# The low parts of split weights, and the one-hot products of the expert selection, on VectorE in place of GpSimd

## The chip, the cores and the metric

The kernel runs on one core of one Trainium2 chip. The metric is the device time of one execution in microseconds; the time before is the median of three runs. The profile shows one execution, with TensorE as PE (its weight loads as PEld), VectorE as DVE, ScalarE as ACT, GpSimd as POOL and the load queue of SyncE as SP.

## What is computed

One layer of a step for 1024 prompt tokens and 8 samples of 8 tokens, in float32. The mixer splits `xn @ w_in` into a differential attention and a gated recurrence; cross attention over 256 memory tokens follows; then every token picks experts:

```
s = einsum('thcd,hckd->thck', q, sub_keys)
s1, i1 = top_k(s[:, :, 0], 16);  s2, i2 = top_k(s[:, :, 1], 16)
cand_s = s1[..., :, None] + s2[..., None, :]
cand_i = i1[..., :, None] * 128 + i2[..., None, :]
top_s, j = top_k(cand_s, 16)
e = take_along_axis(cand_i, j);  g = softmax(top_s)
act = gelu(einsum('ted,td->te', u[e], x))
out = einsum('te,ted->td', g * act, v[e])
```

There are 8 heads with 16 experts each for a token, out of 16384 experts with one row of 1024 numbers in `u` and one in `v`. The samples also attend to 8192 cached tokens, read by pages.

## The kernel before

The 1024 prompt tokens are eight tiles of 128 (0 to 7), the 64 sample tokens are tile S. Matrix products keep float32 precision by splitting both operands into a high and a low part, and adding three products (high x high, high x low, low x high; L290 to L292). For weights this is done on the fly: `raw` [128, 512] is loaded (L284), ScalarE rounds it to the high part (L276) and GpSimd subtracts the high part from `raw` to make the low part (L277, in `split_w`; L306 for a small block; L1326 for the rows of `v`). `raw` has 3 buffers, `ws` (both parts) has 4.

By the profile's clock the program has three stretches, called **stage 1 to 3** here.

- Stage 1, to about 1590 us: projections and mixing of the first groups of tiles, what follows the mixing for tiles 0 and 1, and beside it the samples' attention over the cache (L755 to L798).
- Stage 2, to about 3393 us: what follows the mixing for tiles 2 to 7 and S (`post_pass`), with the mixing of the last groups beside it, and at its end `gates` (L1246 on), which lays out the gates of tiles 2 to 5 for all experts. In `post_pass` each block of queries ends in `peer_select` (L1006): VectorE finds the best 16 of 50 candidates, compares places with `io50` (L1038, `eq`), GpSimd multiplies this one-hot tile with the candidates' expert numbers (L1041, `oh`), VectorE sums (L1043). That is 8 such products for each tile, 72 in all.
- Stage 3, to the end: `dense` (L1279 on). For tiles 2 to 5 all experts are computed, in 16 groups of 8 blocks of 128 experts. For each block `u` is loaded and transposed on TensorE; ScalarE takes the high part (L249), VectorE the low one (L250); 24 products make the scores `S` (L1302); ScalarE applies gelu (L1306), VectorE multiplies by the gates (L1311), ScalarE and VectorE split the result `H` (L1312, L1313). Then two halves of 512 columns: each loads and splits eight `raw` blocks of `v` (L1325, L1326), TensorE multiplies (L1330), and VectorE adds the four banks to `accd` (L1334).

**The gathers.** For tiles 0, 1, S, 6 and 7 the experts' rows are fetched one slot at a time: GpSimd issues an indirect DMA of 128 rows (L1218, 1152 of them), VectorE multiplies a row of `u` with the token and sums it (L1224), or adds a weighted row of `v` to `acc` (L1231). A gathered tile `g` has 3 buffers before stage 3, and 3 + 2 in it. So the next gather waits until VectorE has finished with an earlier one. They run beside the other work in stages 2 and 3.

**The order.** The program is written as streams that are paced against each other by costs in numbers, and a scheduler turns this into one fixed order of instructions for each engine; every engine works its own order from front to back. Gathers are put behind what GpSimd has been given last:

```
with tc.issue_after(gmark[0]):
    return all(next(gstream, False) for _ in range(n))
```

`gmark[0]` is set to the newest instruction at several places, L277 and L1041 among them; the others are L231, L660 and L1271.

Of the kernel before, what the change touches and what calls it, by code (L numbers as in the profile page):

```python
# [7 lines left out]
F32 = mybir.dt.float32  # L8
# [5 lines left out]
OP = mybir.AluOpType  # L14
AX = mybir.AxisListType

P = 128
# [4 lines left out]
S = 8                                   # index of the sample tile (64 tokens)  # L22
# [3 lines left out]
PSLOT = {S: "s", 0: 0, 1: 1, 2: 2, 3: 3, 4: 0, 5: 1, 6: 2, 7: 3}       # slot of a tile's transposed operands  # L26
GORDER = [0, 1, S, 6, 7]                # experts' rows gathered for these tiles
DENSE = [2, 3, 4, 5]                    # all experts' products for these
RATIO = 1.2                             # the sample's attention per unit of other work
LEAD = 100.0                            # work of group 2 before the sample's attention is done  # L30
GRATE = 0.85                            # gathers per unit of other work,
GSLOW = 0.3                             # while experts are chosen
PCOST, MCOST, GCOST, SCOST = 124.0, 160.0, 160.0, 240.0     # work after the mixing, of mixing, of gates, after it with the sample
# [4 lines left out]
def host_consts():  # L38
# [4 lines left out]
    le = (i[:, None] <= i[None, :]).astype(float)          # [j, i] = j <= i  # L43

    def cum(idx):                                          # columns: sum of j <= idx
        return (i[:, None] <= np.asarray(idx)[None, :]).astype(float)
# [23 lines left out]
    c["caus"] = np.where(i[None, :] > i[:, None], NEG, 0.0)    # [q, k]  # L70
# [35 lines left out]
CSEG = [(0, 16), (1, 8), (2, 5), (3, 4), (4, 3)]          # first rank, how many second ranks  # L106
# [3 lines left out]
def step_kernel(ctx: ExitStack, tc: tile.TileContext, consts, a, outs):  # L110
# [25 lines left out]
    stream = [""]                       # whose PSUM banks are handed out  # L136
# [44 lines left out]
    def bcast(src, n):                  # a DRAM vector on every partition  # L181
        return bass.AP(tensor=src.tensor, offset=src.offset, ap=[[0, P], [1, n]])

    # gains of the q/k norms
# [7 lines left out]
    # gains of normed rows, by feature [partition, block]  # L192
# [11 lines left out]
    # lambda  # L204
# [20 lines left out]
    # ---------------------------------------------------------------- helpers  # L225
    def rstd(pool, ss, n, w, k, tag="rs", bufs=4):
        """(ss / k + eps) ** -0.5 for [n, w]."""
        ms = pool.tile([P, 16], F32, tag="ms", name="ms", bufs=3)
        nc.vector.tensor_scalar(ms[:n, :w], ss, 1.0 / k, EPS, op0=OP.mult, op1=OP.add)  # L229
        r = pool.tile([P, 16], F32, tag=tag, name=tag, bufs=bufs)  # L230
        gmark[0] = nc.gpsimd.tensor_tensor(r[:n, :w], ms[:n, :w], nhalf[:n, :w], op=OP.pow).ins  # L231
        return r

    def row_norm(pool, src, n, out, g=None):
        """out = rmsnorm(src) (* g), rows of 1024."""
# [9 lines left out]
    def split_T(dst, blk, ps, n, w, g=None):  # L245
        """PSUM [128, w blocks, n], times the features' gains, into the parts of a transposed operand."""
# [15 lines left out]
    def make_T(t, src, n, g0=0, ng=2, gn=None):  # L262
        """[n, 512 ng] -> parts [128, 2, 8, n] with features on partitions, from block 4 g0."""
# [8 lines left out]
    def split_w(ws, raw, w, g=None):  # L272
        """Parts of weights [128, w], times their rows' gains."""
# [3 lines left out]
        gmark[0] = nc.gpsimd.tensor_tensor(ws[:, 1, :w], raw, ws[:, 0, :w].bitcast(F32), op=OP.subtract).ins  # L277

    def proj(tiles, T, wsrc, c0, w, consume, gn=None):
        """consume(t, ps) for each tile's [n, w] block of columns from c0."""  # L280
# [18 lines left out]
    def proj_ga(tiles, T, wsrc, c0, consume):  # L299
        """consume(t, ps) with ps [16, n]: the gates' low-rank input with features on partitions."""  # L300
# [5 lines left out]
        nc.gpsimd.tensor_tensor(ws[:, 1, :P], raw[:, :P], ws[:, 0, :P].bitcast(F32), op=OP.subtract)  # L306
# [12 lines left out]
    # ---------------------------------------------------------------- long-lived tiles  # L319
    kT, v_all = {}, {}              # prompt keys [4 maps x 32, tile, pair, token] by fours of tiles, values by tile  # L320
# [9 lines left out]
    # ================================================================ mixing  # L330
    def proj_input(tiles):
        """Transposed normed inputs of a group."""
# [10 lines left out]
    def proj_pass(pool, T, cols, L, started):  # L343
        """Projections of the columns cols from the transposed inputs T, kept in L."""
# [122 lines left out]
    def gla_out(wp, t, L, n, srcs, om):  # L467
        """om [n, 512] from the heads' outputs srcs[s] [n, 2 pairs, 128] (head 2 * pair + s)."""
# [134 lines left out]
    def diff_norm(wp, n, ps, om, w0=None):  # L603
        """om [n, 512] = rms-normed heads of ps [n, 512], each times its w0."""
# [14 lines left out]
    def attn_prompt(wp, t, L, om, z, wmax, pb):  # L619
# [6 lines left out]
        for h in range(8):  # L626
# [30 lines left out]
            # P1 / l1 - lam P2 / l2 = (P1 - lam l1 / l2 P2) / l1  # L657
# [26 lines left out]
    # ---------------------------------------------------------------- sample attention over the cache  # L684
    def sample_attention(wp):
# [20 lines left out]
        def chained(f):  # L706
            """Issue f's instructions behind the last page load, so that few registers hold page numbers."""
# [5 lines left out]
        def load_k(i):  # L713
            """Issue the loads of segment i's key pages."""
# [89 lines left out]
        # rows (pair j, head, map, query) of each batch to [token, head, 64]  # L804
# [13 lines left out]
    # ================================================================ after the mixing  # L818
    # memory keys and values of the prompt
# [47 lines left out]
    def mk_evac(dst, pt):  # L867
        """Transposed keys with the gain of the queries."""
# [4 lines left out]
    def cross_softmax(wp, n, ps, r, p):  # L873
        """p [n, 512] = softmax rows of two heads' scores [n, 2, 256], r the queries' 1/rms [n, 2]."""
# [12 lines left out]
    def cross_prompt(wp, g, cqT, r, dst, mkT, mv):  # L887
        """Two heads' attention over the memory."""
# [21 lines left out]
    def cross_sample(wp, cqT, r, dst):  # L910
        # r [64, 4] to rows (32 h + q) of each batch
# [10 lines left out]
        for b in range(8):  # L922
# [45 lines left out]
            # [d, c, (h, 32)] -> parts [d, (h c), 8 b + q]  # L968
# [37 lines left out]
    def peer_select(wp, t, p, v16, i16, r, tv, ef, io50):  # L1006
        """Best 16 of heads 2p and 2p + 1 by the sums of their lists v16 [n, 2 heads x 2, 16] times r: values and experts."""
# [28 lines left out]
        for h in range(2):  # L1036
# [4 lines left out]
            gmark[0] = nc.gpsimd.tensor_tensor(oh[:n], eq[:n].rearrange("p c r -> p r c"),  # L1041
                                    ce[:n, h].unsqueeze(1).broadcast_to([n, 16, 50]), op=OP.mult).ins
# [17 lines left out]
    def post_pass(tiles, oT, side="left", sel=None, sbp=None):  # L1060
        """Everything after the mixing for these tiles, oT their transposed mixer outputs."""
        ptl = [t for t in tiles if t != S]
        with mkpool("post", side) as wp:
# [11 lines left out]
            # cross attention  # L1075
# [46 lines left out]
        with mkpool("post2", side) as wp:  # L1122
# [14 lines left out]
            # PEER queries, scores and selection  # L1137
# [57 lines left out]
    def peer_gather(wp, t):  # L1195
        """Rows of u and v by expert; the sample's 64 tokens take two halves of the slots."""
# [42 lines left out]
    # ---------------------------------------------------------------- all experts for the tiles in DENSE  # L1239
    ND = len(DENSE)  # L1240
    NG = 4 * ND                                          # groups of 32 tokens
    Wd = dram.tile([32, P, NG, P], F32, name="Wd")       # gates [b // 4, a, tokens // 32, (b % 4, tokens % 32)], expert 128 a + b

    def gates(wp, t, io8):
        """The gates of a tile's tokens for all experts, by products of one-hot rows."""
# [37 lines left out]
    def dense(xp, wp, hp, zp):  # L1283
# [9 lines left out]
        for b0 in range(0, P, 8):  # L1293
# [25 lines left out]
            for c0 in (0, 512):  # L1319
                po = [bank("po") for _ in DENSE]  # L1320
                for n, b in enumerate(range(b0, b0 + 8)):
# [4 lines left out]
                    nc.gpsimd.tensor_tensor(vs[:, 1], raw, vs[:, 0].bitcast(F32), op=OP.subtract)  # L1326
# [11 lines left out]
    # ================================================================ the program  # L1338
# [4 lines left out]
    def fin(t, oT, omd, omg):  # L1343
        """The mixers' outputs, transposed."""
# [226 lines left out]
```

## Time and profile before

| | |
|---|---|
| median of three runs | 5152.9 us (5145.41 to 5157.88) |
| span of the profiled execution, first to last instruction | 5142.8 us |
| its own time | not given beside the span; the runs are 2.6 to 15.1 us above the span |
| busy: PE, DVE, ACT, POOL | 84%, 68%, 44%, 58% of the span |
| moved by DMA | 1311.36 MB, 255 GB/s |

A share of the span says little here, since the three stages have different limits. The rows that matter are given by stage below. In a group of instructions the columns are: line, engine, operation, output<-inputs, shapes, count, then the busy time in us and the mean of one in ns, then the engine's idle time just before them with what ended it.

### The profile page before, as it was taken

The page shows a single profiled execution, that of the slowest core. Times are in us where ns is not written, and L with a number is a line of the kernel's source. Part 1 is how long each engine was busy: PE and PEld are TensorE (multiplying, and loading weights), DVE is VectorE, ACT ScalarE, POOL GpSimd, SP SyncE. Part 2 cuts the span into 40 slices and gives each one's busy share as a digit, 9 for nine tenths or more (in the row PEclk, how much of TensorE's full clock was granted, in tenths as well). Part 3 has the DMA queues.
Part 4 walks back from the last instruction along what each step waited for, and adds up shares of the span by engine and source line. Part 5 has one row for each costly group of instructions (what it writes and reads, how often), then busy time and mean ns, then how long its engine had stood idle before and what let it go on. Part 6 is the DMA issues. An engine that isn't in the chain of part 4 may idle for free.

```text
span 5142.8 us, 74353 instructions
## 1 busy us (share of the span) xinstructions
PE 4335.1 (84%) x24048; PEld 3154.7 (61%) x24048; DVE 3514.7 (68%) x6750; ACT 2250.7 (44%) x4954; POOL 2961.8 (58%) x2241
## 2 busy tenths in 40 slices
PE   7999998999998666877872777858889999999998
PEld 5655565565665444553452667746667777777776
DVE  2342127443336689777789976897778888888888
ACT  4565665565565333443332776722222222222221
POOL 4202325520335787764677855556567877777777
PEclk9999999999999787888885888979999999999999
DMA  6678886777676774777765777777889998988998
GB/s 183 211 250 258 279 277 218 244 224 224 206 248 198 257 232 153 236 262 264 255 199 171 219 239 239 223 237 265 274 286 329 318 332 309 319 310 312 329 322 288
DMA packets 562870, 1311.36 MB, mean 255 GB/s; under 512 B 63856, under 2 KB 136752, under 8 KB 557616
## 3 DMA queue, kind: packets, MB, share of 16 engines
q1 hardware_dynamic: 382800, 677.97, 41.1%
q0 software_dynamic: 165888, 604.05, 34.7%
q10 hardware_dynamic: 13792, 24.58, 1.3%
q8 instruction: 190, 3.11, 0.2%
q14 instruction: 200, 1.64, 0.1%
HBM read 1243.54 MB, written 62.59 MB: 254 GB/s over the span
## 4 chain that ended last, share of the span: by engine, by line
issue 14%; DVE 13%; POOL 12%; DMA 12%; PE 6%; ACT 2%; POOLq 0%; SPq 0%; DVEq 0%; ACTq 0%
POOL g L1218 8%; DMA g<-in_peer_v,e 7%; POOL ws L1326 3%; DVE acc L1231 3%; DVE g L1224 3%; DMA g<-in_peer_u,e 2%; PE S L1302 2%; DMA Wd<-wst 1%; PE wb L1275 1%; PE po L1330 1%; POOL ws L277 1%; DVE woa L1268 1%; ACT wob L1271 1%; DVE ef L1043 1%; DVE tmp L1002 0%
## 5 line engine op out<-in xcount | busy, mean ns | idle before, releaser
L277 POOL TENSOR_TENSOR ws<-raw,ws 128x512 fp32r<-128x512 f32 x544 | 730.6, 1355 | 531.4 <-ACT ws L276 451.9
L1231 DVE SCALAR_TENSOR_TENSOR acc<-g,dots,acc 128x1024 f32<-128x1024 f32 x576 | 885.9, 1538 | 209.4 <-DMA g<-in_peer_v,e 203.0
L1224 DVE CUSTOM_DVE_ANT_0 g<-g,xn 128x1024 f32<-128x1024 f32 x576 | 861.7, 1508 | 243.8 <-DMA g<-in_peer_u,e 240.0
L1218 POOL DMA_INDIRECT g<-in_peer_v,e x576 | 719.7, 1249 | 527.1 <-DVE acc L1231 299.6
L1218 POOL DMA_INDIRECT g<-in_peer_u,e x576 | 758.2, 1316 | 414.5 <-DVE dots L1224 228.2
L1302 PE MATMUL S<-xTd,uT 128*128 128x512 f32 x3072 | 803.5, 405 | 76.7 <-DVE uT L250 68.4
L1330 PE MATMUL po<-ws,H 128*128 128x512 f32 x3072 | 780.8, 401 | 67.6 <-ACT H L1312 38.6
L1302 PEld LDWEIGHTS S<-xTd,uT 128*128 128x128 f32 x3072 | 585.0, 193 | 217.3 <-DVE uT L250 85.4
L1330 PEld LDWEIGHTS po<-ws,H 128*128 128x128 f32 x3072 | 572.6, 191 | 197.9 <-ACT H L1312 42.9
L276 ACT CAST ws<-raw 128x512 fp32r<-128x512 f32 x544 | 332.5, 622 | 271.4 <-DMA raw<-in_peer_w_q 66.3
L755 PEld LDWEIGHTS tk<-cst,kp 128*128 128x128 f32 x2048 | 230.3, 141 | 294.9 <-issue 148.7
L758 ACT COPY kt<-tk 128x512 f32<-128x512 f32 x512 | 291.5, 589 | 237.9 <-PE tk L755 202.5
L755 PE MATMUL tk<-cst,kp 128*128 128x128 f32 x2048 | 341.2, 285 | 52.1 <-DMA kp<-in_cache_diff_k 34.2
L1326 POOL TENSOR_TENSOR ws<-raw,ws 128x512 fp32r<-128x512 f32 x256 | 365.0, 1428 | 25.7 <-ACT ws L1325 19.0
L1325 ACT CAST ws<-raw 128x512 fp32r<-128x512 f32 x256 | 159.0, 622 | 449.2 <-DMA raw<-in_peer_v 222.0
L759 PE MATMUL pS<-kt,qbd 128*32 128x512 f32 x1024 | 326.2, 616 | 7.1 <-ACT p L772 5.4
L1275 PE MATMUL wb<-wob,woa 128*128 128x128 f32 x1024 | 263.7, 424 | 74.3 <-ACT wst L1277 41.6
L1275 PEld LDWEIGHTS wb<-wob,woa 128*128 128x128 f32 x1024 | 252.0, 335 | 86.4 <-ACT wst L1277 47.6
L231 POOL TENSOR_TENSOR rs<-ms,nhalf 128x1 f32<-128x1 f32 (+7 forms) x78 | 121.9, 1566 | 315.5 <-DVE ms L229 306.8
L291 PE MATMUL accP<-ws,T 128*128 128x512 f32 x480 | 226.9, 473 | 76.0 <-POOL ws L277 75.9
L291 PE MATMUL acc<-ws,T 128*128 128x512 f32 x608 | 263.4, 434 | 17.5 <-POOL ws L277 17.3
L292 PE MATMUL acc<-ws,T 128*128 128x512 f32 x608 | 249.2, 411 | 9.4 <-DVE T L255 9.4
(427 smaller groups left out, 7733.8 us busy)
## 6 DMA issues: line engine op xcount, KB each, us to landing
kp<-in_cache_diff_k SPq DMA_DIRECT2D x512, 256.0 KB
vp<-in_cache_diff_v SPq DMA_DIRECT2D x512, 256.0 KB
raw<-in_peer_v SPq DMA_DIRECT2D x256, 256.0 KB
u<-in_peer_u SPq DMA_DIRECT2D x128, 512.0 KB
raw<-in_w_in SPq DMA_DIRECT2D x192, 256.0 KB
raw<-in_peer_w_q SPq DMA_DIRECT2D x128, 256.0 KB
Wd<-wst SPq DMA_DIRECT2D x16, 2048.0 KB
W<-Wd SPq DMA_DIRECT2D x32, 1024.0 KB
```

The lines of the kernel that those rows point to most:

```text
L276: nc.scalar.copy(ws[:, 0, :w], raw)
L277: gmark[0] = nc.gpsimd.tensor_tensor(ws[:, 1, :w], raw, ws[:, 0, :w].bitcast(F32), op=OP.subtract).ins
L291: nc.tensor.matmul(o, lhsT=T[t][:, 0, k, :n], rhs=ws[:, 1, :w], start=False, stop=False)
L755: nc.tensor.transpose(out=pt[:, pg * P:(pg + 1) * P], in_=kp[pg][:, j * P:(j + 1) * P], identity=ident)
L759: nc.tensor.matmul(pS[32 * j:32 * j + 32, :w], lhsT=qbd[:, j, b], rhs=kt, start=True, stop=True, tile_position=(0, 32 * j))
L1218: nc.gpsimd.indirect_dma_start(out=g, out_offset=None, in_=src, in_offset=bass.IndirectOffsetOnAxis(ap=e[:, s:s + 1], axis=0))
L1224: nc.vector.tensor_tensor_reduce(out=g, in0=g, in1=xn, op0=OP.mult, op1=OP.add, scale=1.0, scalar=0.0, accum_out=dots[:, s:s + 1])
L1231: nc.vector.scalar_tensor_tensor(acc, g, dots[:, s:s + 1], acc, op0=OP.mult, op1=OP.add)
L1275: nc.tensor.matmul(ps[:, k], lhsT=oa[:, :, 4 * q4 + k], rhs=ob[:, :, 4 * q4 + k], start=True, stop=True)
L1302: nc.tensor.matmul(ps, lhsT=uT[:, i, k], rhs=xT[:, j, k], start=(k + i + j == 0), stop=(k == 7 and j == 1))
L1326: nc.gpsimd.tensor_tensor(vs[:, 1], raw, vs[:, 0].bitcast(F32), op=OP.subtract)
L1330: nc.tensor.matmul(po[m], lhsT=H[n][:, i, c], rhs=vs[:, j], start=(n + i + j == 0), stop=(n == 7 and i == 1))
```

## The change

The subtraction that makes the low part (L277, L306, L1326) and the product with the one-hot tile (L1041) are written with `nc.vector` in place of `nc.gpsimd`. Operands and results are the same. L277 and L1041 no longer set `gmark[0]`. The rest of the diff takes comments out and is not shown.

```diff
     def split_w(ws, raw, w, g=None):
...
         nc.scalar.copy(ws[:, 0, :w], raw)
-        gmark[0] = nc.gpsimd.tensor_tensor(ws[:, 1, :w], raw, ws[:, 0, :w].bitcast(F32), op=OP.subtract).ins
+        nc.vector.tensor_tensor(ws[:, 1, :w], raw, ws[:, 0, :w].bitcast(F32), op=OP.subtract)
...
     def proj_ga(tiles, T, wsrc, c0, consume):
...
-        nc.gpsimd.tensor_tensor(ws[:, 1, :P], raw[:, :P], ws[:, 0, :P].bitcast(F32), op=OP.subtract)
+        nc.vector.tensor_tensor(ws[:, 1, :P], raw[:, :P], ws[:, 0, :P].bitcast(F32), op=OP.subtract)
...
     def peer_select(wp, t, p, v16, i16, r, tv, ef, io50):
...
-            gmark[0] = nc.gpsimd.tensor_tensor(oh[:n], eq[:n].rearrange("p c r -> p r c"),
-                                    ce[:n, h].unsqueeze(1).broadcast_to([n, 16, 50]), op=OP.mult).ins
+            nc.vector.tensor_tensor(oh[:n], eq[:n].rearrange("p c r -> p r c"),
+                                    ce[:n, h].unsqueeze(1).broadcast_to([n, 16, 50]), op=OP.mult)
...
     def dense(xp, wp, hp, zp):
...
-                    nc.gpsimd.tensor_tensor(vs[:, 1], raw, vs[:, 0].bitcast(F32), op=OP.subtract)
+                    nc.vector.tensor_tensor(vs[:, 1], raw, vs[:, 0].bitcast(F32), op=OP.subtract)
```

Three places show how the orders move. First GpSimd in stage 3, in the second half of the experts' groups, before the change: the low parts `ws` stand between the gathers of `v`.

```order
L1326 TENSOR_TENSOR ws<-raw,ws 128x512
L1218 DMA g<-in_peer_v,e 128x1024 x4
L1326 TENSOR_TENSOR ws<-raw,ws 128x512 x3
L1218 DMA g<-in_peer_v,e 128x1024 x5
L1326 TENSOR_TENSOR ws<-raw,ws 128x512
L1218 DMA g<-in_peer_v,e 128x1024 x5
```

With the change GpSimd has nothing but gathers there, to its end:

```order
L1218 DMA g<-in_peer_v,e 128x1024 x62
L1218 DMA g<-in_peer_u,e 128x1024 x128
L1218 DMA g<-in_peer_v,e 128x1024 x128
L1218 DMA g<-in_peer_u,e 128x1024 x128
L1218 DMA g<-in_peer_v,e 128x1024 x128
```

So no gather of stage 3 stands behind a subtraction any more.

Second, VectorE in stage 3, in the second half of the eighth group of eight blocks, before the change (`acc` is the product of a gathered row, `accd` the sum of a bank):

```order
L1231 SCALAR_TENSOR_TENSOR acc<-g,dots,acc 128x1024
L250 TENSOR_TENSOR uT<-pt,uT 128x512
L1231 SCALAR_TENSOR_TENSOR acc<-g,dots,acc 128x1024
L1311 TENSOR_TENSOR hx<-hx,W 128x512
L1313 TENSOR_TENSOR H<-hx,H 128x512
L1231 SCALAR_TENSOR_TENSOR acc<-g,dots,acc 128x1024 x9
L1334 TENSOR_TENSOR accd<-po,accd 128x512 x3
L1231 SCALAR_TENSOR_TENSOR acc<-g,dots,acc 128x1024
L1334 TENSOR_TENSOR accd<-po,accd 128x512
```

The same place with the change:

```order
L1326 TENSOR_TENSOR ws<-raw,ws 128x512
L1231 SCALAR_TENSOR_TENSOR acc<-g,dots,acc 128x1024 x2
L1326 TENSOR_TENSOR ws<-raw,ws 128x512
L1231 SCALAR_TENSOR_TENSOR acc<-g,dots,acc 128x1024 x2
L1326 TENSOR_TENSOR ws<-raw,ws 128x512 x2
L1231 SCALAR_TENSOR_TENSOR acc<-g,dots,acc 128x1024 x2
L1326 TENSOR_TENSOR ws<-raw,ws 128x512
L1231 SCALAR_TENSOR_TENSOR acc<-g,dots,acc 128x1024
L1334 TENSOR_TENSOR accd<-po,accd 128x512
L1231 SCALAR_TENSOR_TENSOR acc<-g,dots,acc 128x1024
L1334 TENSOR_TENSOR accd<-po,accd 128x512 x2
```

The low parts now stand between the products, and the run of nine products in a row is broken up. Counted over the whole order, 471 of the 1152 products stood ahead of the first `uT` of stage 3, and 499 do now.

Third, VectorE in stage 2, at the end of the recurrence of a tile of the last group (`ss`, `ms`, `Sst`), with the projections of tiles 4, 5 and S beside it, before the change:

```order
L1231 SCALAR_TENSOR_TENSOR acc<-g,dots,acc 128x1024
L474 TENSOR_REDUCE ss<-sq 128x4
L535 SCALAR_TENSOR_TENSOR Sst_137<-Sst_136,E,acc 128x128 x2
L229 TENSOR_SCALAR ms<-ss 128x4
L1231 SCALAR_TENSOR_TENSOR acc<-g,dots,acc 128x1024
```

and with it:

```order
L1231 SCALAR_TENSOR_TENSOR acc<-g,dots,acc 128x1024
L277 TENSOR_TENSOR ws<-raw,ws 128x512
L1231 SCALAR_TENSOR_TENSOR acc<-g,dots,acc 128x1024
L535 SCALAR_TENSOR_TENSOR Sst_137<-Sst_136,E,acc 128x128 x2
L277 TENSOR_TENSOR ws<-raw,ws 128x512
L229 TENSOR_SCALAR ms<-ssq_27204 128x4
L1231 SCALAR_TENSOR_TENSOR acc<-g,dots,acc 128x1024
L474 TENSOR_REDUCE ss<-sq 128x4
```

A low part `ws` stands behind nearly every product of a gathered row.

## Rows read from the trace of the kernel before

**Rows 1.** Busy time of each engine in stages 1, 2 and 3 (windows)
```profile
core 0: us, PE busy (x) PEld busy (x) DVE busy (x) ACT busy (x) POOL busy (x), PEclk, DMA share, GB/s
0.00:1590.00 1590.00, 1492.87 (x11508) 936.19 (x11509) 604.30 (x1863) 944.96 (x2180) 482.65 (x402) 0.98 0.74 232
1590.00:3393.00 1803.00, 1259.41 (x5378) 941.69 (x5376) 1454.82 (x3075) 859.17 (x1992) 1218.99 (x900) 0.81 0.72 228
3393.00:5143.00 1750.00, 1582.79 (x7164) 1276.83 (x7164) 1455.61 (x1813) 446.54 (x785) 1260.20 (x941) 0.96 0.87 304
```

**Rows 2.** DVE's two longest waits in stage 3: us in total, times, longest
```profile
DVE g L1224 <- DMA g<-in_peer_u,e: 129.3, 101, 3.9
DVE acc L1231 <- DMA g<-in_peer_v,e: 117.1, 72, 4.4
```

**Rows 3.** Chain that ended last, stage 3 alone, share of it by line
```profile
by line: issue 32.9%; POOL g L1218 20.9%; DMA g<-in_peer_v,e 13.4%; POOL ws L1326 9.5%; PE S L1302 4.8%; DVE acc L1231 4.2%; DMA g<-in_peer_u,e 3.5%; PE po L1330 2.8%; DVE g L1224 1.1%; DVE uT L250 0.9%; DMA raw<-in_peer_v 0.7%; DVE hx L131
```

**Rows 4.** Waits in stage 2: of DVE for gathers, of PE for low parts
```profile
DVE g L1224 <- DMA g<-in_peer_u,e: 110.7, 68, 8.0
DVE acc L1231 <- DMA g<-in_peer_v,e: 85.9, 61, 4.1
...
PE accP L291 <- POOL ws L277: 75.9, 56, 7.3
```

**Rows 5.** Chain that ended last, stage 2 alone, share of it by line
```profile
by line: issue 8.1%; DMA g<-in_peer_v,e 6.8%; DVE g L1224 6.4%; DMA Wd<-wst 4.2%; DVE acc L1231 4.0%; DMA g<-in_peer_u,e 3.6%; PE wb L1275 3.3%; POOL g L1218 2.7%; POOL ws L277 2.7%; DVE woa L1268 2.3%; ACT wob L1271 1.8%; DVE ef L1043 1.2%
```

**Rows 6.** The moved work on POOL: stage 1, stage 2 (two rows), stage 3
```profile
L277 POOL TENSOR_TENSOR ws<-raw,ws 128x512 fp32r<-128x512 f32 x261 | 336.4, 1301 | 474.2 <-ACT ws L276 412.8 <-PE pS L759 17.1 <-issue 12.1
...
L277 POOL TENSOR_TENSOR ws<-raw,ws 128x512 fp32r<-128x512 f32 x284 | 395.5, 1404 | 62.0 <-ACT ws L276 43.9 <-issue 8.9 <-PE wb L1275 6.2
...
L1041 POOL TENSOR_TENSOR oh<-eq,cse 128x800 f32<-128x800 bf16 x39 | 98.7, 2532 | 17.9 <-DVE ef L1043 12.7 <-DVE eq L1038 4.9
...
L1326 POOL TENSOR_TENSOR ws<-raw,ws 128x512 fp32r<-128x512 f32 x252 | 359.0, 1426 | 25.6 <-ACT ws L1325 19.0 <-issue 1.4 <-DMA raw<-in_peer_v 1.0
```

**Rows 7.** Timeline in stage 3: start us, duration us, engine, instruction
```profile
4011.77 0.68 DVE L1313 TENSOR_TENSOR H<-hx,H 128x512 fp32r<-128x512 f32 x1
4012.37 0.68 DVE L250 TENSOR_TENSOR uT<-pt,uT 128x512 fp32r<-128x512 f32 x1
...
4019.81 1.45 POOL L1326 TENSOR_TENSOR ws<-raw,ws 128x512 fp32r<-128x512 f32 x1
4020.04 1.77 DVE L1313 TENSOR_TENSOR H<-hx,H 128x512 fp32r<-128x512 f32 x1
...
4021.73 1.21 DVE L1224 CUSTOM_DVE_ANT_0 g<-g,xn 128x1024 f32<-128x1024 f32 x1
```

**Rows 8.** Timeline of DVE: two instructions that no POOL subtraction held up
```profile
3131.50 1.28 DVE L1231 SCALAR_TENSOR_TENSOR acc<-g,dots,acc 128x1024 f32<-128x1024 f32 x1
3132.70 1.22 DVE L1268 TENSOR_TENSOR woa<-io,wT 128x1024 f32<-128x1024 bf16 x1
```

**Rows 9.** DVE's groups in stage 3 that read two SBUF tiles
```profile
L1231 DVE SCALAR_TENSOR_TENSOR acc<-g,dots,acc 128x1024 f32<-128x1024 f32 x362 | 554.7, 1532 | 121.6 <-DMA g<-in_peer_v,e 117.1 <-DVE H L1313 0.2
L1224 DVE CUSTOM_DVE_ANT_0 g<-g,xn 128x1024 f32<-128x1024 f32 x320 | 454.6, 1439 | 132.7 <-DMA g<-in_peer_u,e 129.3 <-issue 1.2 <-DMA xn<-xnd 1.0
...
L1313 DVE TENSOR_TENSOR H<-hx,H 128x512 fp32r<-128x512 f32 x128 | 115.2, 900 | 5.2 <-ACT H L1312 2.5 <-issue 1.0
```

**Rows 10.** DVE's groups in stage 2
```profile
L1224 DVE CUSTOM_DVE_ANT_0 g<-g,xn 128x1024 f32<-128x1024 f32 x256 | 407.1, 1593 | 111.1 <-DMA g<-in_peer_u,e 110.7
L1231 DVE SCALAR_TENSOR_TENSOR acc<-g,dots,acc 128x1024 f32<-128x1024 f32 x214 | 331.2, 1548 | 87.8 <-DMA g<-in_peer_v,e 85.9 <-issue 1.0
L1268 DVE TENSOR_TENSOR woa<-io,wT 128x1024 f32<-128x1024 bf16 x64 | 106.0, 1660 | 38.5 <-PE wb L1275 38.5
...
L1043 DVE TENSOR_REDUCE ef<-oh 128x16 f32<-128x800 f32 x38 | 36.9, 972 | 4.1 <-POOL oh L1041 4.1
```

**Rows 11.** Windows: the fastest quarter millisecond of stage 3, columns as in Rows 1
```profile
4000.00:4250.00 250.00, 238.96 (x1120) 193.88 (x1120) 219.72 (x297) 69.85 (x124) 193.12 (x147) 1.00 0.93 332
```

## Prediction

> **What bounds the kernel now.** I read the windows first, cut at the points where the work changes [rows 1]. In stage 1 PE is busy 1493 of 1590 us at a granted clock of 0.98, and DVE only 604. PE is the limit there. In stage 2 PE is busy 1259 of 1803 us and the clock falls to 0.81, the upper level only part of the time; DVE is busy 1455. In stage 3 PE is busy 1583 of 1750 and DVE 1456, and the DMA engines 0.87 of the time: three resources close together.
>
> The waits say what a busy share can't. In stage 3 DVE waits 129.3 + 117.1 = 246 us for gathered rows [rows 2]. With its busy time that is 1702 of 1750 us: DVE works its order from front to back, and either computes or stands in front of a gather that has not landed. In stage 2 the same sum is 1455 + 110.7 + 85.9 = 1652 of 1803 [rows 1, 4]. So in both stages DVE, busy or blocked, sets the pace.
>
> The chain that ended last tells who is late for it. In stage 3 it runs in a loop: GpSimd issues a gather (20.9%), its transfer (13.4 and 3.5%), DVE's product, which frees the buffer (4.2 and 1.1%), and GpSimd again. GpSimd's subtraction `ws` L1326 holds 9.5% of this chain, 166 us, although no gather needs it: it stands between two gathers in GpSimd's order [rows 3].
>
> **What one engine costs the other.** The timeline shows the second effect [rows 7]. DVE's subtraction for `H` takes 0.68 us when it is alone. At 4020.04 the same instruction takes 1.77 us: GpSimd's subtraction ran from 4019.81 to 4021.26, and DVE's ended 0.55 us after that. An instruction of DVE that reads two SBUF tiles stands still while GpSimd runs one. [...]
>
> So the means of DVE's groups hold a hidden loss, and the change takes away its cause. Clean durations are 1.28 us for `acc` and 1.22 for `woa` [rows 8], 1.21 for the product with `u` and 0.68 for `H` [rows 7].
>
> **Stage 3, DVE's own time.** Removed: 362 x (1.532 - 1.28) = 91 us on `acc`, 320 x (1.439 - 1.21) = 73 on `u`'s products, 128 x (0.900 - 0.68) = 28 on `H` [rows 9]; 192 us. Added: 252 low parts [rows 6]. Their nearest row is `H`, the same operation and shape, whose successor starts 0.60 us after it [rows 7]: 252 x 0.60 = 151 us. Moved: the orders put 499 products ahead of this stage in place of 471, so 28 x 1.2 = 34 us go to stage 2. DVE's time falls by 192 - 151 + 34 = 75 us.
>
> **Stage 3, the gathers.** GpSimd's 359 us of subtractions [rows 6] leave the loop. They are 9.5 of the loop's 52.6 points of the chain [rows 3], 18%. The unknown is what DVE's 246 us of waits do: bounds are 246 (none left) and 0 (the transfers are as late as before, with DVE coming earlier). I take the loop's share, 18% of 246 = 44 us. Together 119 us.
>
> Two floors stand below. The fastest quarter millisecond had 1120 matmul records [rows 11]; at that pace the stage's 7164 [rows 1] take 1599 us, 151 less than now. It also had a DMA share of 0.93; the stage's 0.87 x 1750 = 1523 us of transfers take 1637 us at that share, 113 less. The second floor is the nearer one, so I take **-110 us**.
>
> **Stage 2.** Added to DVE: 284 low parts x 0.60 = 170 us; 39 one-hot products of whole tiles and 8 of the sample's [rows 6]. For these no row shows DVE's price; below stands `H` with 0.60 for 512 columns, above `woa` with 1.22 for 1024. The reduction over the same 800 columns takes 0.97 [rows 10], some 0.9 from start to start, and I take that: 42 us. The 28 moved products: 34 us. In all 246 us. Removed: 256 x (1.593 - 1.21) = 98 us, 214 x (1.548 - 1.28) = 57, and 64 x (1.660 - 1.22) = 28 on `woa` [rows 10]; 183 us. DVE gets 63 us more work, and since it is occupied for 92% of the stage, I count all of it.
>
> Against it: `ws` L277 on GpSimd holds 2.7% of the chain here [rows 5], 49 us, and PE waits 75.9 us for it [rows 4]. A low part took 1.40 us in GpSimd's order and stood behind gathers whose buffer was still in use; on DVE it takes 0.68. I take the 49 us as gained; the bounds are 76, if PE never waits for a low part, and a loss, which is the rival below. Of the waits for gathers, 197 us, the loop loses 2.7 of its 26.2 points [rows 5], 10%: 20 us. Sum: 63 - 49 - 20 = **-6 us**.
>
> **Stage 1.** 261 low parts [rows 6] add 157 us to a DVE that is idle for 986 of 1590 us [rows 1]; the cover is this idle time, and no gathers run yet. A low part is ready 0.6 us sooner, but PE is the limit and its waits there are for other things. I take **0**. If the cover were gone because DVE stands at some other wait, the price would be stage 2's 75.9 us over 284 low parts, 0.27 us each: 261 x 0.27 = 70 us. That end goes into the range.
>
> The two edits of `gmark[0]` cost nothing by themselves: gathers may be queued somewhat earlier in GpSimd's order, and the 28 moved products are what comes of it. What is late next in stage 3 is the transfer itself and PE.
>
> **Sum.** -110 - 6 + 0 = -116 us against the span of 5142.8: 5027. The median of the runs is 10 us above that span, and I carry this along: **5037 us**, 2.2% faster. Some 0.2% (10 us) is what a measurement of this kernel can tell from no change.
>
> **Rivals.**
>
> *Transfers take the gain (5110 us).* For it: a DMA share of 0.93 at the best pace [rows 11]; gathers that are issued sooner only wait in the queues. Then stage 3 gains half of DVE's 75 us, 37, and with stage 2's 6 the kernel stands at 5110. Against it: the stage's mean share is 0.87, and the first 600 us are far below the best pace.
>
> *All of it comes through (4907 us).* Stage 3 runs at the pace of its best quarter millisecond, 151 us less, and in stage 2 the added 63 us fall into the 151 us in which DVE is neither busy nor waiting for a gather, so that PE's 76 and the gathers' 20 are gained whole: 247 us, 4906 by the runs. For it: smaller instructions of DVE that I left out were held up as well. Against it: all three resources of stage 3 would have to be used as in its best stretch.
>
> *Slower (5183 us): low parts get stuck on DVE in stage 2.* DVE's order has a low part behind nearly every product of a gathered row, and such a product waits in 129 cases of 470 for 197 us, 1.52 us each [rows 4, 10]. On GpSimd a low part did not have to wait for a landing. PE needs it a few products later, and `ws` has only four buffers. If every second of the 284 low parts makes PE wait those 1.52 us, that is 216 us in place of 76: 140 us lost where I have a gain of 6, DVE's added work within it. With stage 3's -110 the kernel is 30 us slower. It decides from 186 us of PE waits for low parts in stage 2 on (76 now, 27 in my forecast). [...] Against the rival: the moved work is nearly paid for by the stalls that go, and GpSimd, whose order had the low parts behind gathers waiting for a buffer, made PE wait too.
>
> *The change cancels out (5153 us).* Stage 3 loses its gain to stage 2 almost exactly.
>
> **From this to the numbers.** Chances: my forecast 0.47 (its own range 4975 to 5100, from the bounds of the gathers' waits and stage 1's 70 us), transfers take the gain 0.15, all of it 0.12, slower 0.19, cancels out 0.07. Faster: 0.47 + 0.15 + 0.12 = 0.74; the same 0.07; slower 0.19. The range of 4910 to 5195 takes in the first two cases, half of the third, the middle of the slower case and the last; about 0.15 lies outside.
>
> **What would show it.** Right: in stage 3 the means of `acc`, `u`'s product and `H` fall to 1.28, 1.21 and 0.69 us; the low parts cost DVE some 0.69 each; GpSimd's busy time falls by at least the 1190 us of [rows 6]; DVE's waits for gathers fall in stage 3 from 246 to about 200; the stage ends about 110 us sooner after its first product. Wrong: means that stay where they are (then the stalls had another cause); DVE's waits for gathers that grow; or PE waiting more than 186 us for `ws` L277 in stage 2, or with stage 1 no longer 1590 us long.

## The result, and the profile after

The changed kernel takes **4978.98 us** (median of 4 runs, 4959.83 to 4988.75) against 5149.86 for the kernel before on the same chip: a ratio of 0.9664, 95% interval 0.9636 to 0.9691. It is 3.4% faster, where 2.2% was forecast; the time lies inside the range. The profiled execution spans 4979.5 us against 5142.8, 163 less.

Cut at 1590 us as in [rows 1], and then at its own first dense product, the windows of the changed kernel (columns as there) are:

```profile
0.00:1590.00 1590.00, 1485.47 (x11334) 925.75 (x11334) 709.66 (x2125) 937.06 (x2163) 109.16 (x121) 0.98 0.72 230
1590.00:3359.00 1769.00, 1248.88 (x5559) 931.91 (x5551) 1433.67 (x3415) 867.62 (x2004) 716.40 (x593) 0.83 0.74 242
3359.00:4980.00 1621.00, 1541.85 (x7164) 1261.40 (x7164) 1386.33 (x2088) 449.47 (x786) 776.07 (x651) 0.98 0.89 319
```

GpSimd (the fifth busy time) gave up 1360 us over the three stages: 482.65 + 1218.99 + 1260.20 before, 1601.63 now. DVE, which took on all of the moved work, is hardly busier for it: less than before in stages 2 and 3, 105 us more in stage 1, 15 us more in all. By the last matmul of the sample's attention (`pS`, L759) and the first of the dense products (`S`, L1302), the stages last 1582, 1777 and 1621 us, against 1562, 1832 and 1749: **+20, -55 and -128**. Stage lengths below are all cut at these two matmuls.

The DVE groups that answer to [rows 9] and [rows 10], first of stage 3, then of stage 2:

```profile
L1231 DVE SCALAR_TENSOR_TENSOR acc<-g,dots,acc 128x1024 f32<-128x1024 f32 x334 | 427.6, 1280 | 42.4 <-DMA g<-in_peer_v,e 39.9
L1224 DVE CUSTOM_DVE_ANT_0 g<-g,xn 128x1024 f32<-128x1024 f32 x320 | 386.1, 1220 | 66.6 <-DMA g<-in_peer_u,e 61.5 <-DMA xn<-xnd 5.0
...
L1326 DVE TENSOR_TENSOR ws<-raw,ws 128x512 fp32r<-128x512 f32 x252 | 173.0, 687 | 28.7 <-ACT ws L1325 26.4 <-issue 1.7
L1311 DVE TENSOR_TENSOR hx<-hx,W 128x512 f32<-128x512 f32 x128 | 88.0, 689 | 53.1 <-ACT hx L1306 44.6 <-issue 8.3
L1313 DVE TENSOR_TENSOR H<-hx,H 128x512 fp32r<-128x512 f32 x128 | 87.6, 685 | 1.5 <-ACT H L1312 0.7
```

```profile
L1224 DVE CUSTOM_DVE_ANT_0 g<-g,xn 128x1024 f32<-128x1024 f32 x256 | 311.1, 1218 | 103.3 <-DMA g<-in_peer_u,e 102.4
L1231 DVE SCALAR_TENSOR_TENSOR acc<-g,dots,acc 128x1024 f32<-128x1024 f32 x243 | 311.1, 1280 | 56.7 <-DMA g<-in_peer_v,e 55.6 <-DVE ms L229 0.3
L277 DVE TENSOR_TENSOR ws<-raw,ws 128x512 fp32r<-128x512 f32 x284 | 193.3, 691 | 31.5 <-ACT ws L276 29.4 <-DMA raw<-in_cross_w_o 1.4
L1268 DVE TENSOR_TENSOR woa<-io,wT 128x1024 f32<-128x1024 bf16 x64 | 77.7, 1219 | 49.2 <-PE wb L1275 49.1
L1041 DVE TENSOR_TENSOR oh<-eq,cse 128x800 f32<-128x800 bf16 (+1 forms) x46 | 74.2, 1614 | 0.0
...
L1269 DVE TENSOR_TENSOR web<-io,wT 128x1024 bf16<-128x1024 bf16 x64 | 43.5, 682 | 15.4 <-ACT wob L1271 15.3
L1043 DVE TENSOR_REDUCE ef<-oh 128x16 f32<-128x800 f32 (+1 forms) x45 | 43.6, 970 | 0.0
...
L664 DVE SCALAR_TENSOR_TENSOR P<-P,w 128x512 f32<-128x512 f32 (+2 forms) x46 | 29.7, 681 | 0.1
```

Every mean that was swollen has fallen to its clean value: `acc` from 1532 and 1548 ns to 1280, `u`'s product from 1439 and 1593 to 1220, `H` from 900 to 685, `woa` from 1660 to 1219. The moved low parts cost 687 to 691 ns each. The one surprise is `oh`: 1614 ns for the product with a one-hot tile.

DVE's waits in stage 3, then two waits of PE in stage 2:

```profile
DVE g L1224 <- DMA g<-in_peer_u,e: 61.5, 60, 3.7
DVE hx L1311 <- ACT hx L1306: 44.6, 42, 3.6
DVE acc L1231 <- DMA g<-in_peer_v,e: 39.9, 45, 2.4
DVE ws L1326 <- ACT ws L1325: 26.4, 31, 5.2
```

```profile
PE ptP L1169 <- ACT sb L1176: 105.3, 10, 16.0
...
PE accP L291 <- DVE ws L277: 40.0, 31, 3.8
```

The waits for gathers in stage 3 are 101 us where [rows 2] had 246. In their place DVE waits for what ScalarE makes of PE's products (`hx`). In stage 2 PE waits 40.0 us for low parts where [rows 4] has 75.9. The chain that ended last in stage 3 shows the new limit, and so do the windows of three of its quarters of a millisecond:

```profile
by line: PE po L1330 33.1%; PE S L1302 31.7%; issue 9.1%; PE pt L268 4.7%; POOL g L1218 4.5%; DMA g<-in_peer_v,e 3.6%; DVE acc L1231 2.3%; DMA g<-in_peer_u,e 1.5%; DVE g L1224 1.2%; DVE uT L250 1.1%; DVE oh L1041 0.9%; DVE hx L1311 0.7%; DV
```

```profile
4000.00:4250.00 250.00, 249.16 (x1171) 205.06 (x1171) 224.41 (x282) 72.00 (x125) 133.28 (x111) 1.00 0.94 343
4250.00:4500.00 250.00, 249.21 (x1176) 205.69 (x1175) 219.55 (x323) 71.64 (x125) 132.78 (x110) 1.00 0.94 345
4500.00:4750.00 250.00, 249.69 (x1182) 205.68 (x1181) 222.66 (x321) 73.73 (x129) 128.74 (x111) 1.00 0.94 344
```

PE's two groups of products hold 65% of the chain, 7.6% before [rows 3]; the issue of gathers fell from 20.9% to 4.5. PE is busy 249 of 250 us at a granted clock of 1.00, with 1171 to 1182 matmuls where the best quarter before had 1120 [rows 11]. So stage 3 went from a loop around gathers to PE at its limit, but for its start: from 3359 to 3600 us PE is busy 182 of 241 us, at a granted clock of 0.88.

### The profile page after: what moved, and what is told of

Its sections match the earlier page's. It is cut to its first block, busy times and chain, and to the rows that moved or that the text cites. A ratio compares the mean times of both kernels' runs of the same rounds, so it can differ in the third digit from the quotient of the medians.

```text
span 4979.5 us, 74107 instructions
## 1 busy us (share of the span) xinstructions
PE 4276.2 (86%) x24048; PEld 3119.1 (63%) x24048; DVE 3529.7 (71%) x7626; ACT 2254.2 (45%) x4953; POOL 1601.6 (32%) x1365
## 4 chain that ended last, share of the span: by engine, by line
PE 51%; DVE 15%; DMA 15%; issue 8%; ACT 5%; POOL 4%; SPq 1%; POOLq 0%; DVEq 0%; ACTq 0%
PE po L1330 11%; PE S L1302 10%; PE pS L759 5%; DMA g<-in_peer_u,e 5%; DMA g<-in_peer_v,e 4%; PE tk L755 4%; POOL g L1218 3%; DVE g L1224 2%; PE acc L290 2%; PE acc L291 2%; PE px L792 2%; PE acc L292 2%; DVE acc L1231 2%; PE pt L268 2%; DVE oh L1041 2%
## 5 line engine op out<-in xcount | busy, mean ns | idle before, releaser
L1218 POOL DMA_INDIRECT g<-in_peer_v,e x576 | 705.3, 1224 | 930.3 <-DVE acc L1231 653.0
L1218 POOL DMA_INDIRECT g<-in_peer_u,e x576 | 685.6, 1190 | 769.9 <-DVE dots L1224 500.5
L1224 DVE CUSTOM_DVE_ANT_0 g<-g,xn 128x1024 f32<-128x1024 f32 x576 | 697.2, 1219 | 169.9 <-DMA g<-in_peer_u,e 163.9
L1302 PE MATMUL S<-xTd,uT 128*128 128x512 f32 x3072 | 786.7, 399 | 31.6 <-DVE uT L250 19.1
L1231 DVE SCALAR_TENSOR_TENSOR acc<-g,dots,acc 128x1024 f32<-128x1024 f32 x576 | 737.4, 1280 | 99.1 <-DMA g<-in_peer_v,e 95.5
L1330 PE MATMUL po<-ws,H 128*128 128x512 f32 x3072 | 761.7, 395 | 34.2 <-ACT H L1312 28.8
L1302 PEld LDWEIGHTS S<-xTd,uT 128*128 128x128 f32 x3072 | 576.0, 190 | 162.0 <-DVE uT L250 29.5
L277 DVE TENSOR_TENSOR ws<-raw,ws 128x512 fp32r<-128x512 f32 x544 | 370.2, 690 | 243.2 <-ACT ws L276 236.0
L755 PE MATMUL tk<-cst,kp 128*128 128x128 f32 x2048 | 350.0, 287 | 63.7 <-DMA kp<-in_cache_diff_k 46.7
L759 PE MATMUL pS<-kt,qbd 128*32 128x512 f32 x1024 | 331.6, 624 | 3.4 <-ACT kt L758 3.2
L291 PE MATMUL acc<-ws,T 128*128 128x512 f32 x608 | 253.5, 419 | 7.4 <-DVE ws L277 7.0
L292 PE MATMUL acc<-ws,T 128*128 128x512 f32 x608 | 247.6, 408 | 13.4 <-DVE T L255 13.2
L1306 ACT ACTIVATE hx<-S 128x512 f32<-128x512 f32 x128 | 76.4, 598 | 385.3 <-PE S L1302 356.4
L291 PE MATMUL accP<-ws,T 128*128 128x512 f32 x480 | 214.9, 448 | 40.9 <-DVE ws L277 40.0
```

Source lines behind the costliest of these rows:

```text
L277: nc.vector.tensor_tensor(ws[:, 1, :w], raw, ws[:, 0, :w].bitcast(F32), op=OP.subtract)
L291: nc.tensor.matmul(o, lhsT=T[t][:, 0, k, :n], rhs=ws[:, 1, :w], start=False, stop=False)
L292: nc.tensor.matmul(o, lhsT=T[t][:, 1, k, :n], rhs=ws[:, 0, :w], start=False, stop=(k == 7))
L755: nc.tensor.transpose(out=pt[:, pg * P:(pg + 1) * P], in_=kp[pg][:, j * P:(j + 1) * P], identity=ident)
L759: nc.tensor.matmul(pS[32 * j:32 * j + 32, :w], lhsT=qbd[:, j, b], rhs=kt, start=True, stop=True, tile_position=(0, 32 * j))
L1218: nc.gpsimd.indirect_dma_start(out=g, out_offset=None, in_=src, in_offset=bass.IndirectOffsetOnAxis(ap=e[:, s:s + 1], axis=0))
```

## Experiments

The theory has two mechanisms. **Stalls**: a DVE instruction with two SBUF inputs stands still while GpSimd runs a two-input instruction, as `H` did when it took 1.77 us in place of 0.68 [rows 7]. **The queue**: a gather stands behind other work in GpSimd's order, so its rows land late. The rival for each run is that one of them does it all, or neither. Each version ran beside the kernel before, whose medians in these rounds were 5147 to 5152 us; differences between versions of different rounds carry these 5 us.

### The parts alone

Three kernels each take one part of the change, all else as before. The first:

```diff
# dense products only, L1326
-nc.gpsimd.tensor_tensor(vs[:, 1], raw, vs[:, 0].bitcast(F32), op=OP.subtract)
+nc.vector.tensor_tensor(vs[:, 1], raw, vs[:, 0].bitcast(F32), op=OP.subtract)
```

> Only the low parts of stage 3 (L1326) are on VectorE; L277, L306 and L1041 stay on GpSimd and set the marks as before. Theory (stalls of VectorE behind GpSimd's subtractions, and gathers queued behind them, are what went): stage 3 shortens by 100 to 130 us, stages 1 and 2 stay; 5020 to 5050 us, and in stage 3 the means of acc, u's product and H are 1.28, 1.22 and 0.69 us, in stage 2 still 1.55 and 1.59. Rival (the new order of the whole program, with the dropped marks, made the gain): little is left here, 5110 us or more.

5040.73 us (5035.69 to 5044.26), ratio 0.980, interval 0.9767 to 0.9832. Stages 1 and 2 stay at 1563 and 1832, stage 3 takes 1642: -107. Its DVE groups from 3393 to 5000 us, stage 3 without its last 37 us:

```profile
L1231 DVE SCALAR_TENSOR_TENSOR acc<-g,dots,acc 128x1024 f32<-128x1024 f32 x347 | 453.2, 1306 | 49.1 <-DMA g<-in_peer_v,e 46.7 <-DVE uT L250 0.2
L1224 DVE CUSTOM_DVE_ANT_0 g<-g,xn 128x1024 f32<-128x1024 f32 x320 | 385.7, 1218 | 71.3 <-DMA g<-in_peer_u,e 69.6 <-DMA xn<-xnd 1.0
```

In stage 2 of this kernel, where GpSimd's subtractions stayed, the same two take 1556 and 1602 ns. The stalls go where the subtractions go, all but 26 ns on the mean of `acc`.

```diff
# split weights only, L277 (and L306)
-gmark[0] = nc.gpsimd.tensor_tensor(ws[:, 1, :w], raw, ws[:, 0, :w].bitcast(F32), op=OP.subtract).ins
+nc.vector.tensor_tensor(ws[:, 1, :w], raw, ws[:, 0, :w].bitcast(F32), op=OP.subtract)
...
```

> Only the low parts of split_w and of the gates' small block (L277, L306) are on VectorE; L1326 and L1041 stay on GpSimd. Theory: stage 3 stays at some 1750 us with its stalls (acc 1.53 us), stage 2 shortens by 20 to 60 us; 5090 to 5130 us. Rival (stage 1 or 2 holds most of the gain): 5050 us or less. Rival (low parts stuck on VectorE, hidden in the whole change by stage 3's gain): slower than before.

5093.32 us, ratio 0.9909 (0.9875 to 0.9943). Stage 1 takes 1574, +12, and stage 2 takes 1777, -55; there `acc` and `u`'s product fall to 1.32 us each. Stage 3 (1739) keeps its stalls (`acc` 1.58 us).

```diff
# one-hot products only, L1041
-gmark[0] = nc.gpsimd.tensor_tensor(oh[:n], eq[:n].rearrange("p c r -> p r c"),
+nc.vector.tensor_tensor(oh[:n], eq[:n].rearrange("p c r -> p r c"),
...
```

> Only the product with the one-hot tile (L1041) is on VectorE; all low parts stay on GpSimd. The profile of the change shows this product at 1.6 us on VectorE where I had taken 0.9. Theory: on VectorE it costs 47 x 1.6 = 75 us in stage 2 and frees VectorE of some stalls and GpSimd of 2.5 us each; within 25 us of before, 5125 to 5175 us. Rival (it is a good part of the gain): 5110 us or less.

5136.73 us, ratio 0.998 (0.9967 to 0.9994): about 10 us less. Stage 2 is 25 us longer, stage 3 29 shorter; 496 products with gathered rows are done before stage 3, 473 before.

By the medians (5147.12 us for the kernel before beside these runs) the three gains are 106 + 54 + 10 = 170 us, the whole of the change's 171; by the ratios 2.0 + 0.9 + 0.2 = 3.1% of its 3.4%, within the intervals. A last part is `gmark[0]` alone, with the work itself left on GpSimd:

```diff
-gmark[0] = nc.gpsimd.tensor_tensor(ws[:, 1, :w], raw, ws[:, 0, :w].bitcast(F32), op=OP.subtract).ins
+nc.gpsimd.tensor_tensor(ws[:, 1, :w], raw, ws[:, 0, :w].bitcast(F32), op=OP.subtract)
...
```

> The kernel before with one difference: L277 and L1041 stay on GpSimd but no longer set the mark behind which gathers are queued. Rival (the gain comes from gathers that move up in the order): 20 us or more faster, below 5130 us, with more gathers done at the start of stage 3. Theory (stalls and queueing behind subtractions): both stay, so it is within 20 us of before.

5123.71 us, ratio 0.9958 (0.9941 to 0.9976), 23 us less: the marks were not free, and the rival's time came true, though only 5 more products are done ahead of stage 3 (478). Most of it lies in stage 3 (1733), little in stage 2 (1829). It is no fourth term to add: the parts that take the marks away with the work have it within them. So some of their gain, up to these 23 us, can be the order of the gathers and neither of the two mechanisms.

### Giving each cost back alone

Here the change stays, and GpSimd gets work that nobody needs behind every second gather: once subtractions of two SBUF tiles, once writes of zeros, which read nothing.

```diff
# behind every second gather
...
+for _ in range(2):
+    nc.gpsimd.tensor_tensor(jk, cm[:, :220].bitcast(F32), cm[:, 220:440].bitcast(F32), op=OP.subtract)
```

> The change, plus useless work on GpSimd: behind every second gather two subtractions of two SBUF tiles (128x220 each, some 0.65 us) into a scrap tile that nobody reads. 1152 of them, some 750 us of GpSimd in stages 2 and 3. Theory A (VectorE stands still while GpSimd runs an instruction with two SBUF inputs): the means of acc and u's product rise from 1.28 and 1.22 us to 1.4 or more, and the kernel takes 5040 us or more. Theory B (what went was only that gathers queued behind other work on GpSimd): the means stay at 1.28 and 1.22, and this kernel and the one with the memsets lose alike.

5321.37 us, ratio 1.0331 (1.0306 to 1.0355); the 1152 subtractions took GpSimd 1179 us.

```diff
# behind every second gather
...
+for _ in range(5):
+    nc.gpsimd.memset(jk, 0.0)
```

> The same, but the useless work is five memsets of 128x220 (no input, some 0.27 us each) behind every second gather: GpSimd is occupied as long as with the two subtractions, and the gathers queue as long. Theory A: the means stay at 1.28 and 1.22 us and the time is within 30 us of the change's. Theory B: as slow as the kernel with the subtractions, 5040 us or more.

5132.17 us, ratio 0.997 (0.9957 to 0.9983). The useless work on GpSimd, first the subtractions and then the writes:

```profile
L1224 POOL TENSOR_TENSOR jk<-cm 128x220 f32<-128x220 f32 x1152 | 1179.2, 1024 | 42.9
...
L1224 POOL MEMSET jk<- 128x220 f32 x2880 | 826.0, 287 | 110.4
```

DVE's groups from 3393 to 5000 us, in the kernel with subtractions (whose stage 3 runs from 3469 to 5325 us) and then in that with writes (3408 to 5129); the extra lines shift the numbers by 5:

```profile
L1229 DVE CUSTOM_DVE_ANT_0 g<-g,xn 128x1024 f32<-128x1024 f32 x320 | 449.1, 1415 | 94.0 <-DMA g<-in_peer_u,e 92.6 <-DMA xn<-xnd 0.3
L1236 DVE SCALAR_TENSOR_TENSOR acc<-g,dots,acc 128x1024 f32<-128x1024 f32 x246 | 355.0, 1443 | 65.6 <-DMA g<-in_peer_v,e 64.1
...
L250 DVE TENSOR_TENSOR uT<-pt,uT 128x512 fp32r<-128x512 f32 x212 | 142.8, 678 | 1.2 <-ACT uT L249 1.0
```

```profile
L1236 DVE SCALAR_TENSOR_TENSOR acc<-g,dots,acc 128x1024 f32<-128x1024 f32 x306 | 391.5, 1279 | 122.2 <-DMA g<-in_peer_v,e 119.0 <-issue 1.4
L1229 DVE CUSTOM_DVE_ANT_0 g<-g,xn 128x1024 f32<-128x1024 f32 x320 | 387.9, 1219 | 138.2 <-DMA g<-in_peer_u,e 131.4 <-DMA xn<-xnd 3.2 <-issue 2.1
```

DVE's waits in stage 3 with the writes:

```profile
DVE g L1229 <- DMA g<-in_peer_u,e: 131.4, 98, 5.7
DVE acc L1236 <- DMA g<-in_peer_v,e: 130.3, 101, 5.3
```

The writes leave DVE's durations clean, to a nanosecond (`acc` 1279 ns for 1280 in the change, `u`'s product 1219 for 1220), and still cost 153 us: the waits for gathers in stage 3 go from 101 back to 262 us, and stages 2 and 3 to 1832 and 1721. My expectation had this run near the change; it missed. The writes take about what the moved work of stages 2 and 3 took on GpSimd before, 395.5 + 98.7 + 359.0 = 853 us [rows 6], and this kernel is back within 0.3% of the kernel before: with the queue about as full as it was, DVE's exchange of stalls for moved work is worth 28 us in stage 3 and nothing in stage 2 (1749 and 1832 before). So most of the gain hangs on the queue. The writes stand at other places between the gathers than the moved work did, so this split is an approximate one. The subtractions swell the two-input instructions again (`acc` 1443 ns, `u`'s product 1415) but not `uT`, which has one input in PSUM (678), and cost another 189 us. Summed over every DVE instruction that overlapped one of GpSimd's, above the median of the same instruction without overlap, the stalls are 380 us in stages 2 and 3. The subtractions also hold GpSimd 353 us longer than the writes do, so the 189 us are not stalls alone; how they divide was not tried.

### What the new price is made of, and a better version

The one-hot tile was laid out [50 places, 16 ranks] and read across, every 16th element. This lays it out the other way round:

```diff
-io50 = zp.tile([P, 50, 16], BF, tag="io50", name="io50", bufs=1)
+io50 = zp.tile([P, 16, 50], BF, tag="io50", name="io50", bufs=1)
...
-nc.vector.tensor_tensor(oh[:n], eq[:n].rearrange("p c r -> p r c"),
+nc.vector.tensor_tensor(oh[:n], eq[:n],
...
```

> The change, with the one-hot tile laid out as the product reads it: io50 and eq are [16, 50] and the product reads eq without a stride of 16 elements. The comparison then has an operand that is repeated along the last axis. If the stride is what makes the product take 1.63 us in place of 0.9, it falls to 0.85 to 0.95 and the comparison rises from 0.57 to at most 0.95: 72 x 0.35 us = 25 us less on VectorE, 4955 to 4980 us. If the stride is not the cause, the product stays at 1.6 us and the kernel is slower than the change.

4955.97 us (4950.63 to 4972.63), ratio 0.9633 (0.961 to 0.9656). `oh` over the whole kernel, in the change and in this version:

```profile
L1041 DVE TENSOR_TENSOR oh<-eq,cse x72: 1549/1611/1746, 833.3 to 3461.7; 128x800 f32<-128x800 bf16 x64, 64x800 f32<-64x800 bf16 x8
```

```profile
L1041 DVE TENSOR_TENSOR oh<-eq,cse x72: 961/974/990, 834.4 to 3446.1; 128x800 f32<-128x800 bf16 x64, 64x800 f32<-64x800 bf16 x8
```

The median falls from 1611 to 974 ns; that of `eq`, whose second input is now repeated element by element, rises from 561 to 976. The stride is what made the product dear. Net 0.22 us, 72 times, makes 16 us, beside 23 us between the medians. The interval overlaps the change's own, and the stages of the two profiled executions do not show the saving where most of the products are: 1564, 1773 and 1612 us, that is -18, -4 and -8. So what the layout is worth by itself in time is not shown.

Then the pace at which gathers are queued, alone and with the new layout:

```diff
-GRATE = 0.85
+GRATE = 0.78
```

> The change, with GRATE 0.78 in place of 0.85: fewer gathers in stage 2, some 30 to 40 more in stage 3, whose gathers end 60 us ahead of TensorE. If TensorE and the transfers bound stage 3 and VectorE has room there: stage 2 shortens by up to 40 us and stage 3 by nothing, 4945 to 4975 us. If the gathers' transfers bound stage 3 as much as TensorE does, it lengthens by as much: 4970 to 4990.

4967.53 us, ratio 0.965 (0.9631 to 0.9668): 11 us less than the change, with intervals that overlap: undecided. By stage it did not act as expected: stage 2 keeps 1775 us, and stage 3, with 17 more products in it, takes 1603, 18 less.

> The change with two further edits together: the one-hot rows laid out with their 50 entries next to each other, and 0.78 gathers per unit of other work in place of 0.85. Alone they gave 4956 and 4968 us against the change's 4979. Theory (the two act in different places: the first shortens 72 products on DVE by 0.65 us each, the second shifts products with gathered rows from stage 2 to stage 3): both gains add, 12 to 23 us below the change and about 4945 us. Rival (both feed the same slack of DVE in stage 2, so the second adds nothing): 4955 to 4970.

**4910.59 us** (4901.91 to 4914.08, 5 runs), against 5152.14: ratio 0.9539 (0.9519 to 0.956). This is the fastest version, 4.6% under the kernel before and apart from every other by its interval. It beat the expectation: 68 us below the change, where the two edits alone gave 23 and 11. Stage 2 takes 1732 us, where each edit alone left it at 1773 and 1775, and stage 3 takes 1599. PE's wait for low parts in stage 2 halves once more:

```profile
PE accP L291 <- DVE ws L277: 20.6, 21, 1.7
```

Why the two together give twice their sum is open; the surplus lies in stage 2.

> As the run before it, with 0.70 gathers per unit. Theory (DVE and PE are both full in stage 3 by now, so each product shifted there costs 1.2 us at its end): no better than 0.78, 4945 to 4975 us. Rival (stage 2 is still where DVE is short): another 10 us less, about 4935.

4943.46 us, ratio 0.9593 (0.9571 to 0.9615): slower than 0.78, as the theory has it. Stage 2 does not gain (1738), and the 23 products shifted to stage 3 cost 38 us there (1637), 1.65 us each.

```diff
# with the layout and 0.78
-sb = (sbp or zp).tile([P, 4, P], F32, tag="sb", name="sb", bufs=6 if sbp else 2)
+sb = (sbp or zp).tile([P, 4, P], F32, tag="sb", name="sb", bufs=6 if sbp else 3)
```

> As the first of these three, with three buffers in place of two for the scores sb that ScalarE copies out of PSUM, for which PE waits 105 us in stage 2 behind those copies. Theory (ScalarE is late with the copy because it waits for a buffer that the selection on DVE still reads): the wait shrinks by some 30 us and the kernel by 10 to 25. Rival (DVE's selection is the pace there, a third buffer only lets the wait move): within 5 us of the first.

4949.94 us, ratio 0.9617 (0.9597 to 0.9636): 39 us slower than with two buffers, which neither theory had. PE's wait for `sb` in stage 2 does shrink, from 86.4 to 75.1 us, but its waits for what DVE and ScalarE make beside it grow:

```profile
PE ptP L1169 <- ACT sb L1176: 75.1, 10, 17.3
PE wb L1275 <- ACT wst L1277: 74.2, 21, 7.7
PE accP L291 <- DVE ws L277: 44.2, 31, 4.5
```

The two-buffer version has 47.6 and 20.6 us in the last two. But stage 2 (1749) has only 17 of the 38 us between the two profiled executions; 10 lie in stage 1 and 11 in stage 3. Why a third buffer costs this is open. Edits as small as this one give the engines other orders, and no run here tells such a difference from an effect of the buffer itself.

## Why the prediction was right, and where it was off

**The direction and its mechanisms held, their weights did not.** The time lies near the lower edge of the forecast's own range, 4975 to 5100. The stalls were real and left with the subtractions: 192 us were taken for stage 3; by the sum over overlapped instructions used above it was 200 us. The run with subtractions shows the same the other way round: two-input work on GpSimd swelled `acc` by 0.16 us on the mean (1443 ns for 1280). The writes of zeros did not (1279 ns). What it is in the two engines that makes DVE wait is not shown.

**Stage 3, -128 for -110.** DVE's own time went as forecast: 1455.61 - 1386.33 = 69 us less, for 75. The mis-sized term is the step "I take the loop's share, 18% of 246 = 44 us": the waits for gathers fell by 145 us, and with 100 us left of them DVE no longer set the pace. A subtraction between two gathers cost more than its place in the chain: once it was gone, "issue" and the transfers of `v` fell from 32.9 and 13.4% in [rows 3] to 9.1 and 3.6%. The writes of zeros show the price of such work by itself: 101 to 262 us of waits, 100 us of stage 3. The forecast gave the queue 44 us and the exchange of stalls for moved work 75; by the writes it is 100 and 28. That 110 came near 128 is in part luck: the two terms as measured, 69 of DVE's time and 145 of waits, would make 214, and PE ended the gain at 128. Neither floor was one as it was worked out. The transfers took 0.89 x 1621 = 1443 us where 1523 were taken as fixed, and the fastest quarter before, from which PE's floor of 1599 us came, was itself held up: in it PE waited 7 us for DVE, 4 for GpSimd's low parts and 3 for ScalarE. Where 1120 matmuls were taken, 1182 fit. Over the whole stage, though, no version here went below 1599 us.

**Stage 2, -55 for -6.** Mainly two terms. "Removed: 183 us" counted three groups; by the same sum over all overlapped instructions it was 298, the other 115 us in many small ones. Some of these, before the change ([rows 10] has the large ones):

```profile
L1269 DVE TENSOR_TENSOR web<-io,wT 128x1024 bf16<-128x1024 bf16 x64 | 53.2, 834 | 8.8 <-ACT wob L1271 8.8
...
L664 DVE SCALAR_TENSOR_TENSOR P<-P,w 128x512 f32<-128x512 f32 (+2 forms) x46 | 38.7, 877 | 0.4
L1020 DVE TENSOR_TENSOR cse<-csrc 128x64 f32<-128x64 f32 (+9 forms) x125 | 32.8, 317 | 4.2 <-ACT csrc L1013 4.2
```

After, they take 682, 681 and 179 ns. Against this the added work cost more than taken: the low parts 193 us for 170 and the one-hot products 74 for 42, since the value for these came from the reduction, which reads along its rows. The waits for gathers fell by 39 us for 20, PE's for low parts by 36 for 49. With these the same sum reads 193 + 74 + 36 (28 moved products) - 298 - 39 - 36 = -70; the stage gave -55. PE's longest wait there, for `sb`, rose from 80.8 to 105.3 us, so its 36 us cannot be taken as gained whole; beyond that the 15 us between are open.

**Stage 1, +20 for 0.** A stage 1 of another length was one of the prediction's own signs of being wrong, and here it was: the step that took 0 failed. The 20 us are inside the bound of 70, and not by the way that the bound assumed: PE hardly ever waits for a low part there. In the trace of the change SP's queue waits for other work of DVE ahead of the weights' loads (L284), as it did not among its longest waits before, and PE's wait for the sample's keys, which go through the same queue, is 46.7 us for 34.2:

```profile
SPq L284 <- DVE ws L277: 107.0, 81, 6.4
...
SPq L284 <- DVE T L255: 17.2, 10, 8.6
SPq L284 <- DVE m L767: 10.8, 8, 2.8
```

Against this, its wait for the low parts themselves was longer before:

```profile
SPq L284 <- POOL ws L277: 185.6, 122, 9.1
```

Such queue waits stand in every version with L277 on DVE, and stage 1 takes 1564 to 1586 us in these, 1560 to 1564 in the others. But the kernel with the one-hot products alone has 42.5 us of the wait for keys at a stage of 1564, and the new layout has the queue's waits at 1564 too. What adds the 20 us is open.

**The rivals.** "Slower" named 186 us of PE waits for low parts as its point; it was 40 us. The products in front of the low parts waited less than before themselves: 158 us in stage 2 for 197. Work went to the engine that set the pace, and the kernel became 3.4% faster. "Transfers take the gain" falls with the time, 131 us under its 5110, and with PE at 249 of 250 us. "All of it comes through" was 72 us too far: PE's best pace was not kept up in the first 600 us of stage 3, where it is busy 531 us.

## What to carry to other kernels

Price work on an engine that also issues gathers by what stands behind it in that engine's order, not by its own share of the chain: here an equal amount of idle writes between gathers cost 153 us while DVE's `acc` and `u`'s product took as long as without them (1279 and 1219 ns). When a two-input operation sits on GpSimd, compare the same DVE instruction with and without overlap, over all its groups and not the largest alone; moving it to DVE may cost DVE almost nothing on balance (15 us of busy time in all here). Before an instruction changes its engine, look at the strides of its operands, and afterwards set the pacing constants again: layout and pace brought 68 us on top of the change.

## What was not expected of the hardware

A DVE product of 128x800 with a bf16 input read at every 16th element takes 1611 ns at the median, and 974 ns with the elements side by side; on GpSimd the first form took 2532 ns on the mean [rows 6]. Why the step costs this is not shown, and steps between 1 and 16 were not run.

Beside 2880 writes of zeros on GpSimd DVE's `acc` took 1279 ns and `u`'s product 1219, as without them, and two groups of DVE with an input in PSUM stood through GpSimd's subtractions unchanged (means of stage 3: `uT` 683 ns before, 684 after; `accd` 681 and 683). No run added GpSimd instructions with one input.
